# A mixer's channel projections as seven quadrant products over all 1024 steps, with the recurrences fed through DRAM

## The chip, the cores and the metric

The kernel runs on one core of one Trainium2 chip. The metric is the device time of one execution in microseconds; before the change three timed runs gave a median of 1631.3 us (1629.72 to 1633.17).

A core has five engines, each with an instruction queue of its own that it works through in order. TensorE (PE) multiplies matrices from SBUF into PSUM. VectorE (DVE) does arithmetic on tiles, ScalarE (ACT) activation functions and copies, GpSimd (POOL) small work. SyncE (SP) computes nothing here; it issues DMA transfers. The engines wait for one another on semaphores.

## What is computed

One layer of a hybrid decoder on a sequence of 1024 steps with 1024 channels, in float32:

```python
h = rms_norm(x, norm_mix)
proj = h @ w_in                                # 1024 x 8192
xa, ga, q, f, v, g, m_a, m_b = split(proj)     # 1024 channels each
xa = causal_depthwise_conv(xa, conv_w, conv_b)
y_a = rg_lru(xa) * gelu(ga)                    # recurrence h[t] = a[t] h[t-1] + u[t] per channel
o = rms_norm(hgrn2(silu(q), k(f), log_f(f), v), hg_norm)   # 8 heads, state 128 x 128
y_b = o * silu(g)
x = x + (sigmoid(m_a) * y_a + sigmoid(m_b) * y_b) @ w_out
x = x + square(relu(rms_norm(x, norm_mlp) @ w_up)) @ w_down
return rms_norm(x, norm_final)
```

Both recurrences run along the sequence. rg_lru has a 256-wide block matrix product for each of its two gates; hgrn2 works in blocks of steps with products of decay factors.

## The kernel before

**Precision.** Every float32 operand of a large product is split in two float32r tiles, a rounded part H (an ACT copy, L76) and the rest L (a DVE subtraction, L77). A product is then three matmuls, H·H, H·L and L·H (`mm3`, L115 to L117).

**Mixer.** The sequence is cut in two chunks c of T = 512 steps, the channels in four pairs p of two heads (256 channels). For each chunk `first_norm` normalises and transposes four row tiles into `hT`. Then for every pair come `project_v`, `project` of xa, `conv`, `project` of q and f, `rg_lru`, `hgrn` and `gates`, which projects g, mb, ga and ma and merges both branches into `ys`, kept in SBUF. `project` reads two weight tiles of 512 KB (`next_w`: one DMA on SP, one split) and makes 48 matmuls of 512 columns in two PSUM banks. `project_v` makes 96 matmuls of 256 columns. Results are read from PSUM directly by the recurrences, and the states `hcar`, `xcar` and `scar` carry over from the first chunk to the second. So each weight tile is loaded and split twice, once for a chunk. The output projection of the first chunk (`out_proj`, L599) runs between the chunks, that of the second beside `second_norm` after the mixer.

**MLP.** The up-projection already uses seven products in place of eight: a quadrant step of weights A (2 × 2 blocks) and activations B (2 × 2 blocks) is made of the seven products of `PLAN`, 12 matmuls each, with sums of the weights (`sums`, L759 to L762) and of the activations (`combos`, L666 to L669). The names t1, n2, T3 and T4 are such sums. This stage lies between about 1020 and 1310 us of the span, and its tiles are called uX, uY and uZ. The down-projection (dX, dY, dZ) follows to the end.

**Order.** The Tile framework writes the order of each engine's queue: ready instructions by priority, where the priority is the order of the program text, raised by `tc.high_priority`. A buffer that is used again makes the next writer wait for its last reader. All loads and stores of the mixer go through SP's queue, in order; the weight splits have a raised priority (400), rg_lru 300.

## Time and profile before

| | before |
|---|---|
| median of 3 runs | 1631.3 us |
| profiled execution | 1630.48 us |
| its span, first to last instruction | 1628.7 us |
| PE busy / instructions | 1584.9 us / 9240 |
| DVE busy / instructions | 1212.7 us / 1751 |
| ACT busy / instructions | 764.4 us / 1186 |
| POOL busy | 65.8 us |
| granted TensorE clock, mean | 0.996 |
| DMA | 246.51 MB, mean 151 GB/s |

A matmul's busy time runs from its start to the end of its pipeline, so neighbours overlap: what counts is the distance between two starts. The windows view gives each engine's busy time in a stretch of the span, with the number of instructions, the granted clock (1.00 is full speed) and the share of the DMA engines' time.

### The profile page before, as it was taken

What the parts mean: (1) busy time and instruction counts of PE and PEld (TensorE: products, weight loads), DVE (VectorE), ACT (ScalarE), POOL (GpSimd) and SP (SyncE); (2) the same over time, 40 slices, a digit from 0 to 9 for tenths busy, and PEclk for the clock granted to TensorE, in tenths of its full rate; (3) what the DMA queues carried; (4) which work ended last, traced back from release to release, by engine and by line L of the source; (5) the groups of instructions that cost most, each with busy time, mean ns of one, the idle gap of its engine ahead of it and who ended that gap; (6) DMA issues with size and microseconds to landing.
All of it is one profiled execution on the core that took longest, in us unless ns stands there. A gap on an engine that the chain in (4) does not pass through costs nothing.

```text
span 1628.7 us, 23177 instructions
## 1 busy us (share of the span) xinstructions
PE 1584.9 (97%) x9240; PEld 1303.1 (80%) x9240; DVE 1212.7 (74%) x1751; ACT 764.4 (47%) x1186; POOL 65.8 (4%) x99
## 2 busy tenths in 40 slices
PE   7999999999999999999999997999999999999998
PEld 6788788788788788787787876888878878888886
DVE  5975956848764865848759688977777888888876
ACT  4643545435442544436434566766776731222113
POOL 0010100100100000100100100000000000000000
PEclk9999999999999999999999998999999999999999
DMA  6212212122243222222122352666656575666652
GB/s 237 91 66 91 91 66 103 66 91 91 80 167 136 86 78 90 80 78 101 69 91 91 117 207 104 250 246 250 235 233 248 222 269 228 251 244 251 254 203 104
DMA packets 57996, 246.51 MB, mean 151 GB/s; under 512 B 6688, under 2 KB 6816, under 8 KB 47136
## 3 DMA queue, kind: packets, MB, share of 16 engines
q1 hardware_dynamic: 56304, 239.27, 39.3%
q10 hardware_dynamic: 1584, 5.77, 1.0%
q8 instruction: 72, 1.18, 0.3%
q14 instruction: 36, 0.29, 0.1%
HBM read 185.24 MB, written 59.77 MB: 150 GB/s over the span
## 4 chain that ended last, share of the span: by engine, by line
PE 80%; DVE 16%; DMA 2%; issue 1%; ACT 1%; POOL 0%; DVEq 0%; POOLq 0%; SPq 0%; ACTq 0%
PE dX L115 3%; PE uX L115 3%; PE uX L117 3%; PE uX L116 3%; PE dX L116 3%; PE dX L117 3%; DVE wL L77 2%; PE pj_ga L117 2%; PE pj_ga L116 2%; PE pj_ga L115 2%; PE pj_f L117 2%; PE pv L115 2%; PE pv L117 2%; PE pv L116 2%; PE pj_ma L117 2%; PE pj_ma L116 2%
## 5 line engine op out<-in xcount | busy, mean ns | idle before, releaser
L77 DVE TENSOR_TENSOR wL<-raw,wH 128x1024 fp32r<-128x1024 f32 x160 | 194.3, 1214 | 150.0 <-ACT wH L76 145.8
L76 ACT CAST wH<-raw 128x1024 fp32r<-128x1024 f32 x160 | 167.9, 1050 | 168.1 <-issue 66.4
L963 DVE TENSOR_TENSOR acc<-acc,dX 128x512 f32<-128x512 f32 x128 | 85.2, 684 | 31.2 <-PE dX L117 30.1
L76 ACT CAST wA<-q 128x512 fp32r<-128x512 f32 x32 | 19.8, 621 | 129.6 <-PE dX L117 103.7
L963 DVE TENSOR_TENSOR acc<-acc,dY 128x512 f32<-128x512 f32 x64 | 43.6, 686 | 17.3 <-PE dY L117 15.7
L345 DVE RECIPROCAL rr<-rr 128x512 f32<-128x512 f32 x16 | 53.5, 3347 | 0.0
L823 ACT ACTIVATE b<-b 128x512 f32<-128x512 f32 x48 | 30.2, 631 | 38.6 <-DVE b L822 38.5
L115 PE MATMUL pv<-wH,hT0H 128*128 128x256 f32 x128 | 37.4, 292 | 0.0
L116 PE MATMUL pv<-wL,hT0H 128*128 128x256 f32 x128 | 37.0, 289 | 0.0
L117 PE MATMUL pv<-wH,hT0L 128*128 128x256 f32 x128 | 37.0, 289 | 0.0
L115 PE MATMUL pv<-wH,hT1H 128*128 128x256 f32 x128 | 36.5, 285 | 0.0
L117 PE MATMUL pv<-wH,hT1L 128*128 128x256 f32 x128 | 36.2, 283 | 0.0
L116 PE MATMUL pv<-wL,hT1H 128*128 128x256 f32 x128 | 36.2, 283 | 0.0
L311 DVE SCALAR_TENSOR_TENSOR xc<-xp,pvt,xc 128x512 f32<-128x512 f32 x48 | 33.1, 746 | 0.0
L551 ACT ACTIVATE on<-po 128x128 f32<-128x128 f32 x64 | 17.0, 278 | 33.5 <-PE po L541 33.2
L570 ACT ACTIVATE smb<-pj_mb 128x512 f32<-128x512 f32 x16 | 9.6, 598 | 45.3 <-PE pj_mb L117 45.2
L824 ACT ACTIVATE b<-b 128x512 f32<-128x512 f32 x48 | 30.1, 630 | 1.1
L77 DVE TENSOR_TENSOR wA<-q,wA 128x512 fp32r<-128x512 f32 x32 | 22.0, 687 | 9.9 <-ACT wA L76 9.7
L444 POOL TENSOR_SCALAR seg<-seg 128x128 f32<-128x128 f32 (+1 forms) x16 | 14.5, 905 | 361.1 <-DVE seg L384 361.1
L565 ACT ACTIVATE g<-pj_g 128x512 f32<-128x512 f32 x16 | 9.6, 600 | 37.2 <-PE pj_g L117 37.2
L384 DVE TENSOR_TENSOR seg<-seg 128x128 f32<-128x128 f32 (+2 forms) x96 | 26.7, 307 | 0.2
L117 PE MATMUL pj_ga<-hT1H,wL 128*128 128x512 f32 x64 | 26.5, 414 | 0.0
(1854 smaller groups left out, 5261.5 us busy)
## 6 DMA issues: line engine op xcount, KB each, us to landing
raw<-wts_in SPq DMA_DIRECT2D x160, 512.0 KB, 3.4
q<-mlp_in SPq DMA_DIRECT2D x64, 512.0 KB, 3.9
x<-x_in SPq DMA_DIRECT2D x8, 512.0 KB, 6.1
acc<-x ACTq DMA_DIRECT2D x8, 512.0 KB, 6.1
y_out<-acc SPq DMA_DIRECT2D x16, 256.0 KB, 2.1
xs<-x_in SPq DMA_DIRECT2D x8, 256.0 KB, 3.5
x<-xs SPq DMA_DIRECT2D x8, 256.0 KB, 2.3
x2s<-x_in SPq DMA_DIRECT2D x4, 512.0 KB, 4.7
```

Of the source, the lines that this page charges most:

```text
L76: keep(A.copy(h, src))
L77: keep(V.tensor_tensor(out=lo, in0=src, in1=h.bitcast(F32), op=ALU.subtract))
L115: PE.matmul(o, ah, bh, start=first, stop=False, **how)
L116: PE.matmul(o, ah, bl, start=False, stop=False, **how)
L117: PE.matmul(o, al, bh, start=False, stop=last, **how)
L311: V.scalar_tensor_tensor(xc[:, s, :], xp[:, j : j + T], pvt[:, PV_CW + 8 * j + u : PV_CW + 8 * j + u + 1], xc[:, s, :], op0=ALU.mult, op1= ...
L345: V.reciprocal(rec, rec)
L384: mul = lambda o, a, b: V.tensor_tensor(out=o, in0=a, in1=b, op=ALU.mult)
L551: A.activation(on[:, 4 * s + n, :], po[:, n * P : (n + 1) * P], AF.Square, accum_out=ssq[:, 4 * s + n : 4 * s + n + 1])
L823: A.activation(b[:, at, :], b[:, at, :], AF.Relu, scale=-1.0 if at == 2 else 1.0)
L824: A.activation(b[:, at, :], b[:, at, :], AF.Square)
L963: V.tensor_tensor(out=dst, in0=dst, in1=banks[bk, pr], op=op)
```

## The change

The mixer no longer walks over chunks and pairs. All eight row tiles are normalised and transposed first; the two halves of the channels and of the steps make the quadrants B11, B21, B22 and B12, and `combos` makes t1, n2, T3 and T4 of them. The v projection is made for both chunks and both halves of its columns at once, in matmuls of 512 columns, and goes to DRAM.

The other seven projections become 28 quadrant products of the MLP's kind (`MIX`): a product takes 256 weight columns and all 1024 steps. XA(p) holds the two heads of xa of a pair, QF(u) holds q and f of one head, GM(u) g and mb, GA(u) ma and ga. The products of a head's gates come two heads later than its recurrence (`_mixer_quads`). Of the four weight sums two come out of DMA transfers: block A21 is loaded to SBUF by SP, and a DMA issued by POOL adds A22 or A11 to it (`added`); DVE makes the other two. The three banks of a product (X, Y, Z) all come from the four banks `pj`, which are read out at once: X after step 0 is copied to Z, and steps 1 and 2 are copied to SBUF.

What leaves PSUM goes to DRAM, head by head: raw xa, q and f (`raw_out`), the finished gates (`gate_a`, `gate_b`), the states of rg_lru (`h_d`) and the normalised outputs of hgrn (`o_d`). `gated_recurrence(p)` and `hgrn(u)` load their inputs from there and run over all 1024 steps, in single buffers that both share by tag (q1, qa, seg, f, kk, v, ks, scT). `merge(u)` loads the four results of a head, merges and splits them and stores `y_d`, which both output projections load again. The first one now stands after the mixer, ahead of the second.

In rg_lru the DVE reciprocal is replaced by an ACT exponential and two DVE steps, the first tap of the convolution moves from ACT to DVE, and in hgrn the scaling by the norm moves from DVE to ACT. Evictions and weight preparation have priority 1000. The pool `raw` has three buffers in place of four.

The diff, cut to its core:

```diff
+ROWS = {"XA": ("xa", "xa"), "QF": ("q", "f"), "GM": ("g", "mb"), "GA": ("ma", "ga")}
+def _mixer_quads():
+    todo = []
+    for p in range(NPAIR):
+        todo.append(("XA", p))
+        for u in (2 * p, 2 * p + 1):
+            todo.append(("QF", u))
+            if p > 0:
+                todo += [("GM", u - 2), ("GA", u - 2)]
+    return todo + [(kind, u) for u in (2 * NPAIR - 2, 2 * NPAIR - 1) for kind in ("GM", "GA")]
+MIX = _mixer_quads()
+UP = len(MIX)
+DOWN = UP + QUADS
...
+        def load(k):
+            if adding and k == 0:
+                raw[k] = pools[0].tile([P, 512], F32, tag="a11", name=f"q{i}{k}")
+                nc.sync.dma_start(raw[k], quads[i, k][:, 0:512])
+            else:
+                raw[k] = raws(f"q{i}{k}")
+                nc.sync.dma_start(raw[k], quads[i, k])
+        def added(k):
+            s[k] = raws(f"s{i}{k}")
+            nc.sync.dma_start(s[k][:, 0:512], halves(quads[i, 0])[1])
+            G.dma_start(s[k][:, 0:512], halves(quads[i, 1 - k])[1 - k], accum_op=ALU.add)
...
+        def sums():
+            a11, (a12, a22) = raw[0][:, 0:512], halves(raw[1])
+            if not adding:
+                s.update({k: raws(f"s{i}{k}") for k in range(2)})
+            (s1, s2), (s3, s4) = halves(s[0]), halves(s[1])
+            if not adding:
+                a21 = raw[0][:, 512:1024]
+                V.tensor_tensor(out=s1, in0=a21, in1=a22, op=ALU.add)
+                V.tensor_tensor(out=s3, in0=a21, in1=a11, op=ALU.add)
+            V.tensor_tensor(out=s2, in0=s1, in1=a11, op=ALU.add)
+            V.tensor_tensor(out=s4, in0=s2, in1=a12, op=ALU.add)
...
+    def transposed(r):
+        c, tt = divmod(r, 4)
+        b = st.tile([P, 2, T], F32, tag=f"b{c}", name=f"hraw{r}", bufs=4 if c == 0 else 1)
+        for h in range(2):
+            pt = bank("hg", f"xT_{r}_{h}")
+            for k in range(4):
+                PE.transpose(pt[:, k * P : (k + 1) * P], xns[r][:, (4 * h + k) * P : (4 * h + k + 1) * P], ident)
+            op_split(pt, f"B{h + 1}{c + 1}", tt)
+            keep(A.copy(b[:, h, :], pt))
+        if c == 0:
+            b0[tt] = b
+        else:
+            a = b0[tt]
+            combos(a[:, 0, :], a[:, 1, :], b[:, 1, :], b[:, 0, :])
+            for src, o in ((a[:, 0, :], "t1"), (b[:, 1, :], "n2"), (b[:, 0, :], "T3"), (a[:, 1, :], "T4")):
+                op_split(src, o, tt)
...
+                        mm3(pp[tt], hh[:, ku % 4, cut], hl[:, ku % 4, cut], wh[:, cols], wl[:, cols], ku == 0, ku == 7)
...
+        for tt in range(4):
+            vt = st.tile([P, 512], F32, tag="vt", name=f"vt{c}{hf}{tt}", bufs=2)
+            A.copy(vt, pp[tt])
+            nc.sync.dma_start(v_d[hf][:, :, 4 * c + tt, :], vt.rearrange("p (h d) -> p h d", h=4))
...
+    w_end[0] = 2 * V_TILES
+    project_v(0, 0, next_rows(4, 5))
+    project_v(0, 1, next_rows(6, 7))
+    project_v(1, 0, small_stuff)
+    project_v(1, 1, lambda: None)
+    for n in range(2):
+        work[n] = quad_steps(n, (w1m, wp), singles=1, adding=True)
+        for k in ("load0", "add0", "add1", "load1", "sums", "a", "b", "c") if n == 0 else ("load0", "add0", "add1"):
+            work[n][k]()
...
+    def gated_recurrence(p):
+        xp = [mt(t, f"xp{2 * p + s}", (P, 1792)) for s, t in enumerate(("q1", "qa"))]
         for s in range(2):
...
+            G.memset(xp[s][:, 0:3], 0.0)
+            nc.sync.dma_start(xp[s][:, 3 : S + 3], xa_d[2 * p + s])
+        wi = mt("v", f"wi{p}", (P, 2, T))
+        raw = wi.rearrange("p s t -> p (s t)")
+        nc.sync.dma_start(raw, wts[V_TILES + p])
+        wh, wl = (mt(t, f"rg{p}{t}", (P, 1024), F32R) for t in ("ks", "scT"))
+        split(raw, wh, wl)
...
-            V.reciprocal(rec, rec)
...
+                A.activation(e, w, AF.Exp, scale=sp4n[:, u : u + 1])
+                A.activation(w, w, AF.Tanh, scale=sp4[:, u : u + 1])
+            for s in range(2):
+                w, ig, e, t = parts[s]
+                V.tensor_scalar(w, w, 0.0, None, op0=ALU.max)
+                V.tensor_scalar(e, e, 1.0, None, op0=ALU.add)
+                V.scalar_tensor_tensor(t, w, 1.0, e, op0=ALU.add, op1=ALU.mult)
+                V.scalar_tensor_tensor(t, t, -4.0, e, op0=ALU.add, op1=ALU.mult)
+                V.tensor_scalar(e, t, -0.5, -1.0, op0=ALU.mult, op1=ALU.add)
...
+                V.scalar_tensor_tensor(w, w, -0.5, t, op0=ALU.mult, op1=ALU.mult)
+                V.tensor_tensor(out=ig, in0=ig, in1=w, op=ALU.mult)
+                h = w
+                V.tensor_tensor_scan(h, e, ig, hcar[:, u : u + 1], op0=ALU.mult, op1=ALU.add)
+                if c + 1 < NC:
+                    G.tensor_copy(hcar[:, u : u + 1], h[:, T - 1 : T])
+                nc.sync.dma_start(h_d[u][:, at : at + T], h)
...
+    def hgrn(u):
+        nm = f"{u}"
+        mul = lambda o, a, b: V.tensor_tensor(out=o, in0=a, in1=b, op=ALU.mult)
+        qr = mt("qa", f"qr{nm}", (P, 1792))[:, 0:S]
+        nc.sync.dma_start(qr, q_d[u])
+        f = mt("f", f"f{nm}", (P, S))
+        kk = mt("kk", f"kk{nm}", (P, S))
+        nc.sync.dma_start(f, f_d[u])
+        v = mt("v", f"v{nm}", (P, 8, P))
+        nc.sync.dma_start(v, v_d[u // 4][:, u % 4])
+        scT = mt("scT", f"scT{nm}", (P, 8, P))
+        G.memset(scT, 0.0)
+        seg = mt("seg", f"seg{nm}", (P, 1536))
+        dd = mt("dd", f"dd{nm}", (P, 8, 32))
+        A.activation(kk, f, AF.Sigmoid, scale=-1.0)
+        A.activation(f, f, AF.Sigmoid)
+        A.activation(seg[:, 0:S], qr, AF.Sigmoid)
+        V.tensor_scalar(f, f, omlb[:, u : u + 1], lb[:, u : u + 1], op0=ALU.mult, op1=ALU.add)
+        V.tensor_scalar(kk, kk, omlb[:, u : u + 1], None, op0=ALU.mult)
+        V.tensor_scalar(f, f, F_MIN, 1.0, op0=ALU.max, op1=ALU.min)
+        q1 = mt("q1", f"q1{nm}", (P, 1792))[:, 0:1536].rearrange("p (a b) -> p a b", b=3)
         r2 = lambda a: a.rearrange("p (a b) -> p a b", b=2)
...
+        mul(q1[:, :, 0:2], r2(seg[:, 0:S]), r2(qr))
...
-        mul(on, on, rs.unsqueeze(2).to_broadcast([P, 8, P]))
...
+                A.activation(on[:, n, :], po[:, n * P : (n + 1) * P], AF.Identity, scale=r[:, n : n + 1])
+            pt = bank("hg", f"poT{half}{u}")
+            for n in range(4):
+                PE.transpose(pt[:, n * P : (n + 1) * P], on[:, n, :], ident)
+            ot = m.tile([P, T], F32, tag="o", name=f"ot{half}{u}", bufs=1)
+            A.activation(ot, pt, AF.Identity, scale=pvt[:, PV_HG : PV_HG + 1])
+            nc.sync.dma_start(o_d[u][:, half * T : (half + 1) * T], ot)
...
+    def merge(u):
+        for c in range(NC):
+            at = slice(c * T, (c + 1) * T)
+            t = {}
+            for k, src in (("h", h_d), ("a", ma_d), ("o", o_d), ("b", mb_d)):
+                t[k] = ev.tile([P, T], F32R if k in "ab" else F32, tag="g", name=f"mg{k}{u}{c}", bufs=3)
+                nc.sync.dma_start(t[k].bitcast(F32) if k in "ab" else t[k], src[u][:, at])
+                if k in "ab":
+                    tf = t[k].bitcast(F32)
+                    V.tensor_tensor(out=tf, in0=tf, in1=t["h" if k == "a" else "o"], op=ALU.mult)
+            a, b = t["a"], t["b"]
+            af, bf = a.bitcast(F32), b.bitcast(F32)
+            V.tensor_tensor(out=af, in0=af, in1=bf, op=ALU.add)
+            A.copy(b, af)
+            V.tensor_tensor(out=a, in0=af, in1=bf, op=ALU.subtract)
+            nc.sync.dma_start(y_d[u, c][:, 0:T], bf)
+            nc.sync.dma_start(y_d[u, c][:, T : 2 * T], af)
...
+    def raw_out(n, step, o, dst):
+        t = ev_tile("t", f"r{step}_{n}", 4)
+        if step == 3:
+            A.copy(t, o)
+        elif step == 4:
+            V.scalar_tensor_tensor(t, o, -1.0, e_of.pop((n, 1)), op0=ALU.mult, op1=ALU.subtract)
+        elif step == 5:
+            V.tensor_tensor(out=t, in0=o, in1=e_of.pop((n, 2)), op=ALU.add)
         else:
...
+            A.activation(t, o, AF.Identity, scale=-1.0)
+        i, j = {3: (0, 0), 4: (1, 1), 5: (0, 1), 6: (1, 0)}[step]
+        nc.sync.dma_start(dst[i][:, j * T : (j + 1) * T], t)
...
+    def gate_b(n, u, step, o):
+        t = ev_tile("t", f"b{step}_{n}", 4)
+        if step == 3:
+            A.activation(t, o, AF.Sigmoid)
+            mul_to(t, t, o)
+            held[n, 0] = t
+        elif step == 4:
+            V.tensor_tensor(out=t, in0=o, in1=e_of.pop((n, 1)), op=ALU.add)
+            A.activation(t, t, AF.Sigmoid, scale=-1.0)
+            held[n, 1] = t
+        elif step == 5:
+            V.tensor_tensor(out=t, in0=o, in1=e_of.pop((n, 2)), op=ALU.add)
+            s = ev_tile("t", f"s{step}_{n}", 4)
+            A.activation(s, t, AF.Sigmoid)
+            mul_to(s, s, t)
+            mul_to(s, s, held.pop((n, 1)))
+            nc.sync.dma_start(mb_d[u][:, T : 2 * T], s)
+        else:
+            A.activation(t, o, AF.Sigmoid, scale=-1.0)
+            mul_to(t, t, held.pop((n, 0)))
+            nc.sync.dma_start(mb_d[u][:, 0:T], t)
+    def gate_a(n, u, step, o):
+        t = ev_tile("t", f"a{step}_{n}", 4)
+        root = 0.044715**0.5
+        if step == 3:
+            A.activation(t, o, AF.Sigmoid)
+            held[n, 0] = t
+        elif step == 4:
+            V.tensor_tensor(out=t, in0=o, in1=e_of.pop((n, 1)), op=ALU.add)
+            s = ev_tile("t", f"s{step}_{n}", 4)
+            A.activation(s, t, AF.Square, scale=root)
+            V.scalar_tensor_tensor(s, s, 1.0, t, op0=ALU.add, op1=ALU.mult)
+            A.activation(s, s, AF.Sigmoid, scale=-2.0 * GELU_C)
+            V.scalar_tensor_tensor(s, t, -1.0, s, op0=ALU.mult, op1=ALU.mult)
+            held[n, 1] = s
+        elif step == 5:
+            V.tensor_tensor(out=t, in0=o, in1=e_of.pop((n, 2)), op=ALU.add)
+            A.activation(t, t, AF.Sigmoid)
+            mul_to(t, t, held.pop((n, 1)))
+            nc.sync.dma_start(ma_d[u][:, T : 2 * T], t)
+        else:
+            A.activation(t, o, AF.Square, scale=root)
+            V.scalar_tensor_tensor(t, t, 1.0, o, op0=ALU.add, op1=ALU.mult)
+            A.activation(t, t, AF.Sigmoid, scale=-2.0 * GELU_C)
+            V.scalar_tensor_tensor(t, o, -1.0, t, op0=ALU.mult, op1=ALU.mult)
+            mul_to(t, t, held.pop((n, 0)))
+            nc.sync.dma_start(ma_d[u][:, 0:T], t)
+    def project(n, step):
+        kind, u = MIX[n]
+        bk, wo, ho = PLAN[step]
+        first = (n, bk) not in banks
+        if first:
+            banks[n, bk] = bank("pj", f"p{kind}{bk}{u}")
+        o = banks[n, bk]
+        wh, wl = ops_w[n][wo]
+        hh, hl = hop[ho]
+        for k in range(4):
+            cols = slice(k * P, (k + 1) * P)
+            mm3(o, wh[:, cols], wl[:, cols], hh[:, k, :], hl[:, k, :], first and k == 0, k == 3, not first)
+        with tc.high_priority(K_EV):
+            if step == 0:
+                banks[n, "Z"] = bank("pj", f"p{kind}Z{u}")
+                A.copy(banks[n, "Z"], o)
+            elif step < 3:
+                e_of[n, step] = ev_tile("e", f"e{step}_{n}", 2)
+                A.copy(e_of[n, step], o)
+            elif kind == "XA":
+                raw_out(n, step, o, (xa_d[2 * u], xa_d[2 * u + 1]))
+            elif kind == "QF":
+                raw_out(n, step, o, (q_d[u], f_d[u]))
+            else:
+                (gate_b if kind == "GM" else gate_a)(n, u, step, o)
...
+    for n, (kind, u) in enumerate(MIX):
+        if n + 2 < UP:
+            work[n + 2] = quad_steps(n + 2, (w1m, wp), singles=1, adding=True)
+        todo = {
+            0: [(n, "d")],
+            1: [(n + 1, "load1")],
+            3: [(n + 1, "sums"), (n + 1, "a"), (n + 1, "b"), (n + 2, "load0"), (n + 2, "add0")],
+            6: [(n + 1, "c"), (n + 2, "add1")],
+        }
+        for step in range(7):
+            project(n, step)
+            with tc.high_priority(K_PREP):
+                for i, k in todo.get(step, ()):
+                    if i < UP:
+                        work[i][k]()
+        if kind == "XA":
+            gated_recurrence(u)
+        elif kind == "QF":
+            hgrn(u)
+        elif kind == "GA":
+            merge(u)
...
+    def load_y(c):
+        ys = [ysp.tile([P, 2, T], F32R, tag="y", name=f"y{u}{c}", bufs=8) for u in range(8)]
+        for u in range(8):
+            nc.sync.dma_start(ys[u].rearrange("p a t -> p (a t)").bitcast(F32), y_d[u, c])
+        return ys
...
+    w_end[0] = len(seq)
+    ys = load_y(0)
+    for hf in range(2):
+        pp = out_proj(ys, hf, range(4), "0")
+        for tt in range(4):
+            cols = slice(hf * 512, (hf + 1) * 512)
+            xs = n2p.tile([P, D], F32, tag="xn", name=f"xs{tt}{hf}", bufs=2)[:, 0:512]
+            nc.sync.dma_start(xs, x[tt * P : (tt + 1) * P, cols])
+            V.tensor_tensor(out=xs, in0=pp[tt], in1=xs, op=ALU.add)
+            nc.sync.dma_start(x2d[tt][:, cols], xs)
+    ys = load_y(1)
...
```

702 lines of the change are left out of this document (294 added, 408 removed).

## The prediction

> **What bounds the kernel now.** I read the page's busy times and its chain of waits first:
>
> ```profile
> span 1628.7 us, 23177 instructions
> ...
> PE 1584.9 (97%) x9240; PEld 1303.1 (80%) x9240; DVE 1212.7 (74%) x1751; ACT 764.4 (47%) x1186; POOL 65.8 (4%) x99
> ...
> PE 80%; DVE 16%; DMA 2%; issue 1%; ACT 1%; POOL 0%; DVEq 0%; POOLq 0%; SPq 0%; ACTq 0%
> ```
>
> PE is busy nearly throughout and carries 80% of the chain; DVE is the only other engine on it. Then the windows view: the mixer, one of its eight rounds (a chunk and a pair), the hottest 20 us of a round, a stall after the mixer, and the up-projection:
>
> ```profile
> 11.00:930.00 919.00, 904.83 (x6302) 756.27 (x6302) 641.70 (x973) 424.86 (x698) 56.98 (x79) 1.00 0.27 95
> 69.20:176.70 107.50, 106.13 (x757) 88.93 (x756) 75.48 (x114) 49.89 (x83) 7.44 (x11) 1.00 0.25 84
> 80.00:100.00 20.00, 18.82 (x299) 14.79 (x300) 19.96 (x45) 6.98 (x11) 3.56 (x6) 1.00 0.18 64
> 980.00:1000.00 20.00, 13.94 (x57) 10.89 (x58) 18.39 (x29) 13.99 (x25) 2.27 (x3) 0.74 0.35 128
> 1030.30:1280.30 250.00, 250.00 (x1072) 200.51 (x1071) 200.64 (x247) 174.93 (x246) 0.00 (x0) 1.00 0.63 244
> ```
>
> Columns are length, then busy time and instructions of PE, weight loads, DVE, ACT, POOL, clock, DMA share, GB/s. The mixer is bound by PE (905 of 919 us), with DVE at 70%; only while a recurrence runs is DVE full (19.96 of 20), and PE still does 18.8, because projections that need no recurrence fill its queue. The last row matters most: the up-projection already works in seven products, with DVE and ACT at 80% and 70%, and PE has no gap. So PE's work is the first thing to count, and whether DVE leaves PE alone the second.
>
> **PE's work.** The timeline of PE gives the distance between two starts, here in the first and last rows of a run of 26 matmuls of 512 columns and of 29 matmuls of 256:
>
> ```profile
> 119.72 0.39 PE L116 MATMUL pj_ma<-hT0L,wH 128*128 128x512 f32 x1
> ...
> 125.39 0.39 PE L117 MATMUL pj_ma<-hT0H,wL 128*128 128x512 f32 x1
> ...
> 126.61 0.28 PE L116 MATMUL pv<-wL,hT0H 128*128 128x256 f32 x1
> ...
> 129.96 0.28 PE L117 MATMUL pv<-wH,hT0L 128*128 128x256 f32 x1
> ```
>
> 5.67/25 = 226.8 ns and 3.35/28 = 119.6 ns. The seven-product form is slower a matmul: 250/1072 = 233.2 ns in the up-projection's window. Counts by group:
>
> ```profile
> L117 PE MATMUL pj_ga<-hT1H,wL 128*128 128x512 f32 x64 | 26.5, 414 | 0.0
> L115 PE MATMUL pv<-wH,hT0H 128*128 128x256 f32 x128 | 37.4, 292 | 0.0
> ```
>
> Removed: 6 such groups of 64 for each of seven projections, 2688 x 0.2268 = 609.6 us. Added: 28 quadrants of 84 matmuls, 2352 x 0.2332 = 548.5 us. That is -61.1 us; at the old distance it would be -76.2. I take the up-projection's, since the form is the same. v: 768 x 0.1196 = 91.9 us become 384 x 0.2268 = 87.1, or 89.5 at 0.2332; I take -4. The gates' block products of rg_lru (192 matmuls), the blocks of hgrn, the transposes and both output projections keep their counts. **PE's work falls by 65 us, by 81 at most.**
>
> The Trainium skill ("TensorE: Matmul & The Clock Gate", "Wait — 56ns, not 53.3ns?") puts warm matmuls of 512 columns 215.7 ns apart; by it the 336 matmuls saved would be worth 72 us. The trace disagrees, with 226.8 and 233.2 ns at clock 1.00, so the rows decide.
>
> **DVE's work.** The rows that carry the prices:
>
> ```profile
> L77 DVE TENSOR_TENSOR wL<-raw,wH 128x1024 fp32r<-128x1024 f32 x160 | 194.3, 1214 | 150.0 <-ACT wH L76 145.8 <-PE pj_ga L117 2.6 <-PE xT_x L145 1.5
> L345 DVE RECIPROCAL rr<-rr 128x512 f32<-128x512 f32 x16 | 53.5, 3347 | 0.0
> L347 DVE TENSOR_TENSOR ri<-ri,xc 128x512 f32<-128x512 f32 x16 | 11.0, 686 | 0.0
> L384 DVE TENSOR_TENSOR on<-on,hrs 128x1024 f32<-128x1024 f32 x8 | 9.8, 1225 | 14.5 <-POOL hrs L557 14.5
> L376 DVE TENSOR_SCALAR f<-f,par 128x512 f32<-128x512 f32 x16 | 8.7, 541 | 0.0
> ```
>
> Weight splits of the mixer: 136 x 1.214 = 165 before; 28 x 3.5 + 16 (v) + 4 (rg) = 118 after, 143 us: -22. Weight sums on DVE: 56 x 0.686 = +38. Evictions of XA and QF: 24 x 0.686 = +16. Gates: a round had 10 operations of 512 columns, 4 of 1024 and a scalar one, about 12.5 us, 100 in all; after, 6 in `gate_b`, 8 in `gate_a` and 8 in `merge` for each head, 176 x 0.686 = 121: +21. Row tiles 4 to 7 get four sums and four splits more each: 32 x 0.686 = +22. Reciprocal: -53.5 + 32 x 0.686 = -31. First tap: 16 x 0.541 = +9, less 3 for the carried columns. Scaling of `on`: -10. Sum **+40 us**. The first output projection, 8 splits and 8 additions or 15 us, leaves the mixer with 192 x 0.2268 = 43.5 us of PE. So DVE has 641.7 + 40 - 15 = 667 us of work in a mixer whose PE work takes 919 - 65 - 43.5 = 810: 82%. That is the up-projection's load, where PE lost nothing.
>
> ACT, by these rows:
>
> ```profile
> L346 ACT ACT_TABLE_LOAD x16 | 20.5, 1283 | 0.3
> L819 ACT COPY e<-uX 128x512 f32<-128x512 f32 x32 | 18.4, 578 | 0.4 <-PE uX L117 0.4
> ```
>
> 84 copies of X, X and Y cost 49 us, the other evictions and repeated sigmoids some 30 more than the ones they replace, and rg_lru needs exp, tanh, sqrt and sigmoid; if each of its eight half-sequences reloads tables four times more, that is 41 us. 425 + 120 = 545 of 810, 67%: not the bound.
>
> **What does not lie beside other work.** (a) PE's first 53 us (9 to start, two halves of v at 22) must see eight row tiles ready; DVE needs 8 x 1.28 for the norms, 48 x 0.69 for their splits and sums and 10 weight splits of 1.21, 56 us in all, so that the last tile may come late: +3, between 0 and 10. (b) Quadrants in hot stretches: 18.8 of 20 us is what PE keeps when DVE is full. The round as a whole loses 1.4 of 107.5, which is in the 919 already; if every stretch were like the hot one, 6% of 549 us, 33. The up-projection's row gives 0. I take +9. (c) After GA7, `merge(7)` goes out and in again:
>
> ```profile
> xs<-x_in SPq DMA_DIRECT2D x8, 256.0 KB, 3.5
> x<-xs SPq DMA_DIRECT2D x8, 256.0 KB, 2.3
> ...
> raw<-wts_in SPq DMA_DIRECT2D x160, 512.0 KB, 3.4
> ```
>
> store 2.3, load 3.5, four operations 2.8, a copy 0.6, store 2.3, load of y 3.4: 15 us. The first output projection needs head 7 only after seven heads' matmuls, 7 x 12 x 0.227 = 19 us, so it hides if heads 0 to 6 are back in SBUF by then; their loads stand in SP's queue behind the merge's, which wait. +5, between 0 and 15. (d) The recurrences' chain, next paragraph: +10, between 0 and 80.
>
> **The chain of recurrences.** The buffers are single, so a pair's `gated_recurrence` and two `hgrn` follow each other. One round before, by DVE's timeline (first rounds), from convolution to gates, from gates to scan, and through hgrn:
>
> ```profile
> 43.85 0.74 DVE L311 SCALAR_TENSOR_TENSOR xc<-xp,pvt,xc 128x512 f32<-128x512 f32 x1
> ...
> 57.36 0.43 DVE L342 TENSOR_SCALAR rw<-rw 128x512 f32<-128x512 f32 x1 [2.26 <-ACT rw L338]
> ...
> 75.50 1.28 DVE L352 TENSOR_TENSOR_SCAN h<-rr,hcar,ri 128x512 f32<-128x512 f32 x1
> ...
> 79.39 0.86 DVE L384 TENSOR_TENSOR q<-q,f 128x512 f32<-128x512 f32 x1
> ...
> 110.64 0.16 DVE L555 TENSOR_SCALAR hssq<-hssq 128x8 f32<-128x8 f32 x1
> ```
>
> 13.5 + 19.4 + 31.4 = 64 us, of which about 12 are other work (ten splits by L77's 1.21) and 4 the saved part of two reciprocals: 48. A pair now needs two of these and three trips through DRAM (2.3 + 3.5): 114 us. PE needs 7 x 19.6 + 48 x 0.227 + 2 x 14 (107.5 less 336 and 96 matmuls and the rg block) = 176 us a pair. Preparation and evictions go ahead of the chain on DVE: seven quadrants of 5.7 and 23 us of gates and evictions, 63 of those 176 us. If they only fill its waits, a pair takes about 160; if all add, 114 + 63 = 177, and in the time in which no matmul of a recurrence slows the quadrants, up to 197. Starting at about 125, four pairs end between 765 and 913, PE's projections at about 790 to 805. So it is nearly even. I take 170, and 10 us of tail.
>
> **Sum**: -65 + 3 + 9 + 5 + 10 = -38; 1630.5 (the profiled execution: span 1628.7 and 1.8 around it) becomes **1592 us**. The median is 0.8 above that execution, which changes nothing here.
>
> **The rivals.** *Only PE counts*: everything hides as in the up-projection, and the sum is -65 to -81: 1550 to 1565, middle 1557. For it: 250 of 250 us at the same DVE load. Against it: there no chain of recurrences had to keep up. Chance 0.22.
>
> *The chain becomes the bound*: at 197 us a pair, 3.3 pairs are done when the projections run out near 780; the rest, 0.7 x 114 = 80 us, runs with PE nearly idle and ends at 860, some 55 late, and the output projection then starts cold, as the window at 980 does (0.74). 1630.5 - 65 + 17 + 55 + 5 = 1643. It costs more than the change saves once a pair takes over 190. For it: DVE at 82%, ACT's table loads, POOL's power function and queues in order lengthen each step. Against it: the hot row. Chance 0.20.
>
> *The weights come late*: A21 plus A22 is two transfers one after the other, about 7 us by the 256 KB row, in the 11 us between `add1` and `sums`; all loads share SP's queue with stores that wait for evictions, where before a load already waited long:
>
> ```profile
> SPq L84 <- DVE wL L77: 670.3, 132, 10.3
> ```
>
> No transfer issued by POOL is in the trace. From 0 (the slack holds) to 3 us a quadrant: 28 x 1.5 = 42 in the middle, 1634: no gain. Chance 0.13.
>
> The Trainium skill ("SBUF — State Buffer", "A bandwidth-pool intuition that's wrong (but worth ruling out)") says that a transfer issued by GpSimd waits for its descriptors while DVE holds the port that both share, 3.1 us in place of 0.62. By it each addition would come 2.5 us later, 1.5 of the 4 us of slack would be left, and this rival would be nearer 0.2; no run here shows such a transfer yet.
>
> **How the numbers follow.** The forecast has 0.45, its own range 1570 to 1620 from the bounds of (a) to (d). The range **1545 to 1650** takes in PE's floor at the old distance (1549) and the chain at 197. A difference under 0.2%, 3.3 us, can't be told from none. Faster: 0.45 + 0.22 + 0.05 from the lower parts of the rivals = 0.72; slower 0.22; same 0.06.
>
> **What would show it.** Quadrant matmuls 233 ns apart and 19.6 us a quadrant; v at 227 ns a matmul. PE above 95% from 11 us to the last GA; DVE near 82% there. `hgrn(7)` ends before GA7 if the forecast holds; a stretch of PE under 50% before the output projection, with DVE full, shows the chain. Waits of DVE or ACT on DMA for s or raw tiles show late weights. Wrong would be: DVE's sum off by over 60 us, since 100% is 143 us away, or PE's distance off by 10 ns, 24 us.

## The result, and the profile after

The changed kernel takes 1700.2 us (median of four runs, 1699.1 to 1703.4) against 1631.1 us before: a ratio of 1.043, 95% interval 1.041 to 1.044. It is slower by 69 us, where 38 us less was forecast. The forecast time, 1592 us, is 108 us off; 107 of these find their place below.

The page after, with the total busy times and the chain of waits:

```profile
span 1697.3 us, 22898 instructions
PE 1563.2 (92%) x8520; PEld 1242.5 (73%) x8520; DVE 1242.3 (73%) x1908; ACT 839.5 (49%) x1335; POOL 128.1 (8%) x169
PE 43%; DMA 11%; DVE 9%; ACT 4%; issue 3%; POOL 1%; SPq 0%; DVEq 0%; POOLq 0%; ACTq 0%
```

PE is busy for 22 us less than before (1584.9), where 65 were forecast; part of the difference is a lower granted clock, as the windows below show. Its share of the chain fell from 80% to 43%. DMA's rose from 2% to 11% and ACT's from 1% to 4%, while DVE's fell from 16% to 9%; the shares of the line add up to 71%, and the rest is not named in it. The windows view by stages, after: the v projection, the 28 quadrants with the recurrences, the stretch from the last gate to the up-projection, the up-projection. The last row is the same for one quadrant without a recurrence beside it.

```profile
9.00:119.90 110.90, 101.70 (x448) 79.85 (x449) 69.88 (x121) 60.75 (x99) 7.00 (x10) 1.00 0.48 152
119.90:919.40 799.50, 726.10 (x4936) 572.46 (x4935) 580.92 (x989) 427.15 (x738) 114.36 (x141) 0.97 0.52 156
919.40:1052.70 133.30, 105.99 (x443) 84.77 (x441) 73.52 (x96) 50.73 (x75) 4.87 (x7) 0.89 0.71 248
1052.70:1375.60 322.90, 316.10 (x1342) 251.59 (x1341) 257.77 (x322) 220.57 (x312) 0.55 (x1) 0.99 0.58 220
833.20:852.80 19.60, 19.60 (x85) 15.79 (x84) 9.81 (x14) 8.07 (x12) 1.81 (x2) 1.00 0.62 183
```

and before, from the last gate to the up-projection:

```profile
926.80:988.50 61.70, 53.24 (x255) 43.38 (x254) 54.49 (x75) 41.33 (x65) 5.93 (x7) 0.94 0.60 217
```

In the 800 us of the quadrants PE is idle for 73 us. What it waits for there, as total, times and longest:

```profile
PE poT L702 <- ACT on L699: 13.2, 11, 2.4
PE sc L536 <- DVE q L506: 13.1, 4, 6.1
PE pr L126 <- ACT xcH L87: 11.3, 5, 4.9
PE sc L536 <- DVE qb L506: 6.9, 4, 3.8
PE sc L621 <- DVE qb L506: 6.7, 4, 2.2
PE pGAX L126 <- DVE a L781: 5.6, 4, 2.6
```

Five of these six are matmuls of a recurrence (hgrn's blocks and outputs, rg_lru's gates) whose operand DVE or ACT had not finished. The sixth is a quadrant that waits for its bank to be read out. None of PE's waits in this window is a quadrant that waits for its weights. And what DVE waits for in the same window:

```profile
DVE s L252 <- DMA s<-quads_in: 50.4, 21, 5.2
DVE s L253 <- DMA q<-quads_in: 24.6, 19, 4.5
```

These are the two weight sums, 75 us. The first (L252) waits for an addition by transfer; the wait of the second (L253) is put down to the plain load of q. The timeline of DVE shows one of them in its place (start, duration, line, operation, and in brackets the idle time before it):

```profile
549.41 1.22 DVE L88 TENSOR_TENSOR ws315L<-s,ws315H 128x1024 fp32r<-128x1024 f32 x1
553.80 0.69 DVE L252 TENSOR_TENSOR s<-s,q 128x512 f32<-128x512 f32 x1 [3.17 <-DMA s<-quads_in]
554.41 0.42 DVE L484 TENSOR_SCALAR xp<-xp 128x512 f32<-128x512 f32 x1
554.74 0.69 DVE L496 TENSOR_TENSOR wi<-wi 128x512 f32<-128x512 f32 x1
...
557.68 1.28 DVE L498 TENSOR_TENSOR_SCAN wi<-xc,hcar,wi 128x512 f32<-128x512 f32 x1
...
565.83 1.22 DVE L88 TENSOR_TENSOR ws116L<-s,ws116H 128x1024 fp32r<-128x1024 f32 x1
```

The sum for quadrant 16 (553.80) is needed by the split at 565.83, 12 us later. DVE stands still for 3.17 us in front of it until the transfer of s lands, with rg_lru's next steps and its scan (L484, L496, L498) queued behind. Over the 28 quadrants the first sum stands 18.6 us ahead of DVE's half of its split in the median (6.6 to 33.7). ACT's half, which reads the sum first, begins 16.0 us after it.

### The profile page after: what moved, and what is told of

Same layout as the page of the kernel before. It is cut to its first block, busy times and chain, and to the rows that moved or that the text cites. A ratio compares the mean times of both kernels' runs of the same rounds, so it can differ in the third digit from the quotient of the medians.

```text
span 1697.3 us, 22898 instructions
## 1 busy us (share of the span) xinstructions
PE 1563.2 (92%) x8520; PEld 1242.5 (73%) x8520; DVE 1242.3 (73%) x1908; ACT 839.5 (49%) x1335; POOL 128.1 (8%) x169
## 4 chain that ended last, share of the span: by engine, by line
PE 43%; DMA 11%; DVE 9%; ACT 4%; issue 3%; POOL 1%; SPq 0%; DVEq 0%; POOLq 0%; ACTq 0%
PE dX L126 3%; PE dX L128 3%; PE dX L127 3%; PE uX L126 3%; PE uX L127 3%; PE uX L128 3%; DMA q<-quads_in 3%; DMA s<-quads_in 2%; PE dY L128 2%; PE dY L126 2%; PE dY L127 2%; PE uY L128 2%; PE uY L126 2%; PE uY L127 2%; DMA raw<-wts_in 1%
## 5 line engine op out<-in xcount | busy, mean ns | idle before, releaser
L241 POOL DMA_DIRECT2D s<-quads_in x56 | 51.5, 920 | 441.0 <-DMA s<-quads_in 124.9
L252 DVE TENSOR_TENSOR s<-s,q 128x512 f32<-128x512 f32 x60 | 41.4, 689 | 56.4 <-DMA s<-quads_in 51.7
L87 ACT CAST wH<-raw 128x1024 fp32r<-128x1024 f32 x40 | 42.0, 1051 | 66.1 <-PE po L127 30.1
L88 DVE TENSOR_TENSOR wL<-raw,wH 128x1024 fp32r<-128x1024 f32 x40 | 48.9, 1223 | 34.8 <-ACT wH L87 34.4
L126 PE MATMUL po<-wH,y 128*128 128x512 f32 x128 | 53.2, 421 | 18.7 <-DMA y<-yd 8.6
L253 DVE TENSOR_TENSOR s<-s,q 128x512 f32<-128x512 f32 x60 | 41.3, 688 | 29.7 <-DMA q<-quads_in 29.5
L88 DVE TENSOR_TENSOR wA<-q,wA 128x512 fp32r<-128x512 f32 x60 | 41.2, 686 | 20.5 <-ACT wA L87 20.5
L1124 DVE TENSOR_TENSOR acc<-acc,dY 128x512 f32<-128x512 f32 x64 | 43.5, 686 | 16.3 <-PE dY L128 15.3
L127 PE MATMUL po<-wL,y 128*128 128x512 f32 x128 | 53.3, 416 | 0.3 <-DVE wL L88 0.3
L128 PE MATMUL po<-wH,y 128*128 128x512 f32 x128 | 52.2, 408 | 0.0
L126 PEld LDWEIGHTS po<-wH,y 128*128 128x128 f32 x128 | 25.5, 200 | 26.0 <-DMA y<-yd 9.0
L127 PEld LDWEIGHTS po<-wL,y 128*128 128x128 f32 x128 | 26.0, 203 | 6.5 <-DVE wL L88 1.3
L702 PE MATMUL poT<-ident,on 128*128 128x128 f32 x64 | 18.4, 313 | 13.2 <-ACT on L699 13.2
L128 PEld LDWEIGHTS po<-wH,y 128*128 128x128 f32 x128 | 25.9, 202 | 5.5
L506 DVE TENSOR_TENSOR kk<-kk,seg 128x768 f32<-128x768 f32 (+1 forms) x32 | 26.9, 840 | 3.2 <-PE sc L639 3.2
```

The source lines that it names most:

```text
L87: keep(A.copy(h, src))
L88: keep(V.tensor_tensor(out=lo, in0=src, in1=h.bitcast(F32), op=ALU.subtract))
L126: PE.matmul(o, ah, bh, start=first, stop=False, **how)
L127: PE.matmul(o, ah, bl, start=False, stop=False, **how)
L128: PE.matmul(o, al, bh, start=False, stop=last, **how)
L241: G.dma_start(s[k][:, 0:512], halves(quads[i, 1 - k])[1 - k], accum_op=ALU.add)
```

## The experiments

All times are beside the kernel before on the same chip, 1630 to 1631 us. Each comes from a single execution unless a median is given. Eleven executions of one kernel below lie between 1622.2 and 1630.8 us, so two single times that are less than 10 us apart are not told apart. "Ahead" always means the median distance from the start of the first sum to DVE's half of its split. "Quadrants" is the time from the first matmul of the first quadrant to the last of the last; 799.5 us in the changed kernel.

**Without the recurrences.** In the main loop the two calls are taken out, and `merge` reads other tensors of the same shape:

```diff
-        if kind == "XA":
-            gated_recurrence(u)
-        elif kind == "QF":
-            hgrn(u)
-        elif kind == "GA":
+        if kind == "GA":
```

> Leaves out both recurrences (gated_recurrence and hgrn are not called; the merge reads raw xa and q in place of their results). What stays is the v projection, the 28 quadrants with all their weight preparation, the gates, the merge and everything behind. Theory A (TensorE's queue is in order, and matmuls of the recurrences whose inputs are late hold the quadrants behind them: 61 of the 73 us of PE waits between 120 and 918 us stand at such matmuls) expects the quadrants at 19.6 us each, 28 x 19.6 + 12 = 561 us from the first to the last in place of 798, and so about 1460 us in all. Theory B (the weight sums come late by themselves, 76 us of DVE waits at L252 and L253) expects the quadrants to stay at 21.5 us or more and the waits on s and q of DVE to stay near 70 us: 600 us or more for the 28, 1500 us or more in all.

Measured: 1491.2 us, quadrants 592 us. The window of the quadrants, then DVE's waits in it:

```profile
120.00:712.00 592.00, 564.96 (x2353) 447.41 (x2352) 270.11 (x351) 212.74 (x312) 46.67 (x53) 0.98 0.60 163
```

```profile
DVE s L253 <- DMA q<-quads_in: 83.7, 27, 6.2
DVE s L252 <- DMA s<-quads_in: 78.8, 26, 4.9
```

Neither expectation holds alone. DVE waits 162 us for transfers at the sums with little else to do, and the quadrants lose 43 us against 28 x 19.6 = 549; the 27 us in which PE is idle are all waits for DVE to read a bank. The rest of the 250 us that the changed kernel has above 549 is the recurrences' own matmuls, and 46 us that only both together cost: 799.5 - 592 = 207.5, of which 161 are PE's additional busy time (726.1 less 565.0).

**The sums on DVE.** The accumulating transfers go; DVE adds instead:

```diff
-            G.dma_start(s[k][:, 0:512], halves(quads[i, 1 - k])[1 - k], accum_op=ALU.add)
-            if not adding:
-                a21 = raw[0][:, 512:1024]
-                V.tensor_tensor(out=s1, in0=a21, in1=a22, op=ALU.add)
-                V.tensor_tensor(out=s3, in0=a21, in1=a11, op=ALU.add)
+            a21 = (s1, s3) if adding else (raw[0][:, 512:1024],) * 2
+            V.tensor_tensor(out=s1, in0=a21[0], in1=a22, op=ALU.add)
+            V.tensor_tensor(out=s3, in0=a21[1], in1=a11, op=ALU.add)
```

> The accumulating transfers that POOL issues are gone: SyncE loads A21 into both sum tiles as before, and DVE adds A22 and A11 (56 more operations of 0.69 us, 38 us of DVE). Theory B (the late accumulation holds DVE in order at the sums, and with it the recurrences' work behind) expects DVE's waits on transfers of s and q to fall from 76 us to under 35, PE's idle time between the first XA and the last GA from 73 us to 15 to 45, and a time of 1640 to 1675 us. Theory A without B (the recurrences' own chain of DVE, ACT and POOL steps is what comes late) expects no gain: 38 us more of DVE in the chain's way, 1700 to 1725 us.

Measured: 1639.8 us, 60 us less than the changed kernel, with 56 operations more for DVE, 38 us by the price of one. The window of the quadrants, then DVE's waits for s and q in it:

```profile
120.00:859.50 739.50, 706.87 (x4936) 559.04 (x4936) 612.10 (x1043) 428.01 (x738) 76.09 (x86) 1.00 0.45 149
```

```profile
DVE s L248 <- DMA q<-quads_in: 7.3, 7, 2.5
DVE s L249 <- DMA s<-quads_in: 6.3, 7, 2.6
```

DVE's waits fall from 75 to 14 us, PE's idle time from 73 to 33 us, and the same 4936 matmuls take 19 us less of busy time at a granted clock of 1.00 in place of 0.97: with 41 us of gaps went 19 us of slow clock. But this edit does two things. The second transfer goes, and the additions now wait for the tile q, so that the sums stand later in DVE's queue: the first is 3.0 us ahead of its split (the second 12.8, where it was 17.8). It does not tell whether the transfer or the place of the sum was at fault.

**The recurrences later.** Each call stands one quadrant later:

```diff
+    due, LATE = [], 6
...
         for step in range(7):
             project(n, step)
+            if step == LATE:
+                while due:
+                    due.pop(0)()
...
         if kind == "XA":
-            gated_recurrence(u)
+            due.append(lambda u=u: gated_recurrence(u))
         elif kind == "QF":
-            hgrn(u)
+            due.append(lambda u=u: hgrn(u))
```

> Each recurrence is written one quadrant later in the program, behind the seven steps of the next quadrant, so that its loads and matmuls stand later in every queue than the planner had them; nothing else changes. Theory A expects fewer waits of PE at recurrence matmuls (61 us to about 30), as their inputs have 20 us more: about 1670 us, if the last recurrence then still ends before the last quadrant. If the order is not the point but each step's inputs come late against its predecessor in the same chain (the lag moves along with the chain), nothing changes: 1690 to 1710 us.

Measured: 1702.3 us, quadrants 798 us. The recurrences did move (the last transposes of an hgrn output start at 848.7 us in place of 827.2), the time did not: PE is still idle for 75 us, and DVE still waits 78 us at the sums. That PE's queue holds matmuls whose operands are late is how the loss shows; this run gives no sign that it comes from there.

**The norms ahead.**

```diff
     rows(0)
     fill_w(1)
     load_x(2)
+    rows(1)
     transposed(0)
-    rows(1)
     fill_w(2)
     load_x(3)
+    rows(2)
     transposed(1)
-    rows(2)
+    rows(3)
     transposed(2)
-    rows(3)
     fill_w(3)
     transposed(3)
...
             for r in rs:
                 load_x(r)
                 rows(r)
+            for r in rs:
                 transposed(r)
```

> Of the eight row tiles, the norm of the next one is written ahead of the transposes of the one before it (in the program order that ACT and DVE are held to), so that square, norm, transposes and splits of two tiles overlap. Theory C (the 20 us that the v stage came late, 120 against some 100 us, lie in this serial chain, 7.7 us a tile with ACT and DVE half idle) expects the first quadrant 10 to 14 us earlier, near 107 us, and 1686 to 1692 us in all. The rival, that the splits of the weights or the matmuls themselves set the pace, expects less than 3 us: 1697 to 1703 us.

Measured: 1695.0 us, between the two ranges; the first quadrant starts at 116.4 in place of 119.9. The chain costs 4 us, not 10 to 14. Most of the 20 us that this expectation wanted to explain were no loss: 384 matmuls of 228 ns, 64 transposes and a start like the one before fill the stage, as the prediction had it.

**No addition at all.** The accumulating transfer is left out, and nothing takes its place.

```diff
-            G.dma_start(s[k][:, 0:512], halves(quads[i, 1 - k])[1 - k], accum_op=ALU.add)
```

> Leaves out the 56 accumulating transfers and puts nothing in their place: both sum tiles hold A21 alone, so the weights s1 to s4 are other numbers than the kernel needs, with the same operations on them. Against the run in which DVE makes these two sums (1639.8 us), it tells what DVE's 38 us cost there. If DVE's load lies beside PE's work (612 of 739 us, 83%), it is within 5 us of that run, 1633 to 1642. If DVE in its order is what now holds the recurrences, it is faster by a good part of the 38 us: 1605 to 1625.

Measured: 1648.7 us, outside both ranges: 51 us less than the changed kernel, and 9 us more than with the 56 additional operations of DVE. Taking that work off DVE brought nothing, so DVE's load is not what counts here. The sum again stands early, 21.9 us ahead of its split, but the sums wait only for plain loads, 26 us in all. In the changed kernel, a sum waits for two transfers in a row, by the first two of these medians from issue to landing:

```profile
s<-quads_in SPq DMA_DIRECT2D x56, 256.0 KB, 2.8
s<-quads_in POOLq DMA_DIRECT2D x56, 256.0 KB, 4.4
q<-quads_in SPq DMA_DIRECT2D x28, 256.0 KB, 4.5
```

The third line is a plain load of the same size, no faster than the accumulating one. So the runs show what the second transfer in the row costs, and not that an accumulating transfer is slow by itself.

**Two steps more.** Sums, splits, loads and additions are written two steps later:

```diff
-        for k in ("load0", "add0", "add1", "load1", "sums", "a", "b", "c") if n == 0 else ("load0", "add0", "add1"):
+        for k in ("load0", "add0", "add1", "load1", "sums", "a", "b", "c") if n == 0 else ("load0", "add0"):
...
         todo = {
-            0: [(n, "d")],
+            0: ([(n, "c")] if n else []) + [(n, "d"), (n + 1, "add1")],
             1: [(n + 1, "load1")],
-            3: [(n + 1, "sums"), (n + 1, "a"), (n + 1, "b"), (n + 2, "load0"), (n + 2, "add0")],
-            6: [(n + 1, "c"), (n + 2, "add1")],
+            5: [(n + 1, "sums"), (n + 1, "a"), (n + 1, "b"), (n + 2, "load0"), (n + 2, "add0")],
         }
```

> The accumulating transfers stay on POOL, but the sums of the next quadrant and the first two splits are written at step 5 in place of 3, the loads and additions that follow them two steps later too, and the splits of s3 and s4 at the first step of their own quadrant: from the issue of the second addition to the sums there are five steps, 14 us, in place of four, 11. If the gain of the sums on DVE came from time (two transfers one after the other plus POOL's issue do not fit in 11 us), DVE's waits on s and q fall from 76 us by a third or more, and the time to 1650 to 1680 us. If it came from the ring of three raw buffers (each tile is loaded when the one before it is split, so that everything moves along), nothing changes: 1690 to 1710 us.

Measured: 1713.2 us, 3 us above the second range, and DVE's waits for s and q are 88 us, not fewer than 75. The place in the text gives the sum no time: it still stands 18.4 us ahead of its split. This spoke for the ring of raw buffers (three tiles that are used in turn, each loaded when an earlier one has been split), so the ring was changed by itself.

**Four raw tiles.** The recurrences are left out, for room, and the ring is one tile longer:

```diff
-        return wp.tile([P, 1024], F32, tag="raw", name=name, bufs=3)
+        return wp.tile([P, 1024], F32, tag="raw", name=name, bufs=4)
```

> Both recurrences left out as in no_rec (their buffers are what makes room), and the ring of raw weight tiles four deep in place of three, 4 KB a partition more; accumulating transfers on POOL as in the changed kernel. Theory R (a raw tile is loaded at the moment in which the split of the tile three places before it frees its buffer: load, accumulation, sum and split stand in one closed ring, so no load is ever ahead) expects DVE's waits on s and q in the 28 quadrants to fall from 168 us to under 90, and the quadrants from 592 us to 555 to 570: 1455 to 1470 us in all. Rival T (two transfers one after the other take longer than the place in the program gives them, whatever the buffers) expects 585 to 592 us for the quadrants and 1485 to 1492 us in all.

Measured: 1487.6 us, quadrants 580 us. DVE's waits:

```profile
DVE s L252 <- DMA s<-quads_in: 131.5, 26, 7.3
DVE s L253 <- DMA q<-quads_in: 44.4, 22, 4.4
```

176 us, not fewer than the 162 with three tiles. The quadrants take 12 us less but begin 8 us later (at 128.2), and the whole gains 3.6 us, which is too little to be told from nothing. So the theory falls: the loads come earlier, and the sums move up with them (20.6 us ahead of the split in place of 10.9). That fits a planner which puts a sum where it takes its transfer to be done. The next run fixes the place.

**The sums tied to step 3.** The transfers stay; the sums take a factor of 1.0 that is made of step 3's product:

```diff
...
-            V.tensor_tensor(out=s2, in0=s1, in1=a11, op=ALU.add)
-            V.tensor_tensor(out=s4, in0=s2, in1=a12, op=ALU.add)
+            if adding and i > 0:
+                one = gates.pop()
+                V.scalar_tensor_tensor(s2, s1, one, a11, op0=ALU.mult, op1=ALU.add)
+                V.scalar_tensor_tensor(s4, s2, one, a12, op0=ALU.mult, op1=ALU.add)
...
+                if step == 3 and n + 1 < UP:
+                    gates.append(const.tile([P, 1], F32, tag="gate", name=f"one{n}", bufs=2))
+                    V.tensor_scalar(gates[0], banks[n, "Z"][:, 0:1], 0.0, 1.0, op0=ALU.mult, op1=ALU.add)
```

> The changed kernel with its accumulating transfers, and one thing more: the two sums that DVE makes for the next quadrant multiply by a 1.0 that is made of the finished product of step 3, so that they can't stand in DVE's queue ahead of that step, where the text has them (28 small DVE operations more, no other edit). Theory P (the planner takes the two transfers to be done sooner than they are and puts the sums, at priority 1000, right behind them, some 20 us before the split needs them, so that DVE waits in order with the recurrences behind it) expects DVE's waits on s and q to fall from 76 us to under 30 and a time of 1640 to 1665 us. If the transfers really come too late for the splits, the waits stay and the weights come later still: 1700 to 1730 us.

Measured: 1653.4 us, as its theory P expected. The window of the quadrants, then DVE's longest waits between 120 and 870 us:

```profile
121.00:875.60 754.60, 703.76 (x4938) 557.37 (x4938) 586.12 (x1015) 431.34 (x741) 109.80 (x141) 0.99 0.56 164
```

```profile
DVE xc L490 <- ACT xc L485: 20.8, 8, 4.3
DVE mga L722 <- DMA mga<-mad: 17.2, 7, 6.5
DVE mgb L722 <- DMA mgb<-mbd: 13.1, 6, 4.2
```

No wait for s or q is among DVE's waits of 2 us or more in that window. The accumulating transfers are all there, so they are in time for the weights; only DVE had been made to wait for them. POOL still issues every one of them, so its queue is not where most of the loss was. That the planner takes the transfers for shorter than they are is argued from this; what the plan assumed is in no trace. The sum now stands 2.2 us ahead of its split. Four runs make a table of two by two:

| | sum early (18.6 and 21.9 us ahead) | sum late (2.2 and 3.0 us ahead) |
|---|---|---|
| accumulating transfer | 1700.2 us, DVE waits 75 us | 1653.4 us |
| plain transfers alone | 1648.7 us, DVE waits 26 us | 1639.8 us, DVE waits 14 us |

Either remedy alone brings 47 to 52 us, and both together 60, though the run at the lower right also has 56 additions more on DVE. Most of the loss needs both the early place and the second transfer.

**The sums without their priority.**

```diff
-            with tc.high_priority(K_PREP):
-                for i, k in todo.get(step, ()):
-                    if i < UP:
+            for i, k in todo.get(step, ()):
+                if i < UP:
+                    with tc.high_priority(K_PREP if k != "sums" else 0):
                         work[i][k]()
```

> The changed kernel, with the sums alone taken out of priority 1000: they are written at the same place with the priority of the program text. If it is the raised priority that puts the sums ahead of the recurrences' work in DVE's queue, DVE's waits on s and q fall under 40 us and the time to 1640 to 1670 us, as with the sums tied to step 3 (1653.4 us). If it is the planner's idea of when the two transfers are done (DVE is free at that moment in its plan, whatever the priority), nothing changes: 1690 to 1710 us.

Measured: 1683.9 us, between the two ranges: the waits for s and q are still 69 us and the sum stands 13.4 us ahead. The raised priority accounts for 16 of the 47 us that tying the sums brought.

**A faster way to the end.** With the sums on DVE and the norms ahead, the first output projection is reordered:

```diff
+    first_proj(0, range(7))
+    first_proj(1, range(4))
     for hf in range(2):
-        pp = out_proj(ys, hf, range(4), "0")
+        first_proj(hf, range(4, 8) if hf else (7,))
+        pp = pps[hf]
```

`first_proj` holds the matmuls of `out_proj`, with the banks of the second half in `sc` and `hg`.

> The two sums on DVE (1639.8 us) and the norms ahead of the transposes (5 us less when done alone), and the first output projection in another order: heads 0 to 6 of its first half, heads 0 to 3 of its second half in the four other banks, then head 7 and the rest, so that 30 us of matmuls in place of 19 stand before the last head is needed. If the stretch from the last gate to the up-projection is long (131 us against 105 before) because head 7's way through DRAM takes some 30 us, the wait of 8.4 us for y and the cold clock behind it go, and the time is 1615 to 1626 us. If the stretch is set by the second norm's chain behind it (stores of x2, loads, norms), the gain is given back there: 1630 to 1637 us.

> The same kernel as dve_v_tail, timed in five rounds: 1623 to 1627 us, a ratio to before of 0.995 to 0.998, if its one look was typical; if it was a lucky one, 1628 to 1633 us and no difference from before that can be told.

Measured: 1624.7 us in a single execution, and 1627.1 us as the median of eleven, a ratio to before of 0.9976, interval 0.9966 to 0.9987. This version is 73 us faster than the changed kernel and level with the one before: 0.24% less, which the interval tells from nothing, but only just. Its median lies between the two outcomes of the first expectation and just above the upper edge of the lower one of the second. The stretch from the last gate to the up-projection fell from 131 us, with the sums on DVE alone, to 125. The wait for y is gone, and another stands in its place:

```profile
PE po L126 <- ACT wH L87: 14.2, 1, 14.2
```

SyncE's timeline shows that weight load (L95) behind loads of y for the second projection and behind the stores (L939) and loads (L937) of the first one's results:

```profile
903.04 0.86 SPq L868 DMA_DIRECT2D y<-yd  x2
907.09 1.03 SPq L939 DMA_DIRECT2D x<-xs  x2
912.01 0.86 SPq L95 DMA_DIRECT2D raw<-wts_in  x2
```

The stores wait for DVE's additions, here as total, times and longest between 880 and 925 us; the loads of y wait for PE for only 0.2 us in that time:

```profile
SPq L939 <- DVE xs L938: 13.5, 7, 4.8
```

**Those weights on another queue.**

```diff
-        nc.sync.dma_start(raw, wts[i])
+        (nc.sync if i < V_TILES else nc.scalar).dma_start(raw, wts[i])
```

> As dve_v_tail (1624.7 us), but the weights of both output projections are loaded by ACT's queue in place of SyncE's, where the last ones stood for 14 us behind loads of y that wait for TensorE. If that queue is the cause of the 14.2 us wait of TensorE for the weights and of the cold clock behind it: 1608 to 1616 us. If the transfers themselves are the limit there (298 to 353 GB/s between 890 and 920 us), the wait goes to y or x and the time stays at 1620 to 1626 us.

Measured: 1631.2 us, the median of ten, ratio to before 1.001 (0.9995 to 1.0025), above both ranges. The wait of 14.2 us is gone and its place is taken again:

```profile
PE xT_h L902 <- DVE xn_h L150: 8.6, 3, 5.0
PE po L127 <- DVE wL L88: 5.5, 2, 5.1
```

The stretch is 122 us long, 3 less, and the total got no better. What sets this stretch was moved twice and not settled. The DMA engines are busy for 0.85 to 0.95 of the time between 890 and 920 us in the version before this one, so the transfers themselves stay a rival that no run tests.

## Why the prediction was wrong, step by step

**PE's work** was right. A quadrant alone takes the 19.60 us that were worked out (84 matmuls, 233 ns each), and with the sums on DVE, at clock 1.00, PE is busy in the quadrants for 706.9 us where the sum has 704. Two rows of the v projection, with sixteen distances between them:

```profile
91.00 0.39 PE L127 MATMUL pv<-wL,hB22H 128*128 128x512 f32 x1
94.66 0.39 PE L128 MATMUL pv<-wH,hB22L 128*128 128x512 f32 x1
```

3.66/16 = 229 ns, between the two distances used. The rule of the Trainium skill ("TensorE: Matmul & The Clock Gate", "Wait — 56ns, not 53.3ns?"), 215.7 ns, does not hold here either.

**DVE's work** was right: 69.9 + 580.9 = 651 us up to the last gate against 667 worked out. ACT's 488 us were put too high, at 545. Neither engine is the bound; the share of DVE in the quadrants is 73%, and at 83% (the sums on DVE) the kernel is 60 us faster.

**(a) The v stage** was right: 11 + 106 (what the sum leaves beside four times 176 us) + 3 = 120; the first quadrant starts at 119.9, and writing the norms ahead took 3.5 us of that away.

**(b) and (d), and the rival of late weights: here it failed.** The sum gave the quadrants 704 + 9 + 10 = 723 us; they took 799.5. Of these 76 us, 45 to 60 go when the wait of the sums is taken away in one way or the other. With the sums on DVE the quadrants take 739.5 us, 16 above the forecast and inside the bounds of (d); where these 16 come from is open.

The step that failed is that the sum puts the wait for the additions at nothing. The prediction had the mechanism as a rival: two transfers in a row, about 7 us. That length was right: from SyncE's load of s to POOL's issue are 3.5 us in the median, and from there to the first sum 4.3. But it counted them against 11 us "between `add1` and `sums`", which is a distance in the text, and the planner does not keep it. 22 of the 28 first sums start 4.0 to 4.5 us after the issue of their addition, that is, right behind the transfer, and two steps more in the text gained nothing. So DVE waits for the transfers, wherever the text puts the two.

It also had another payer in mind. The rival prices what a quadrant loses for lack of weights, and names waits of DVE on transfers for s as the sign. The sign came, but the weights were in time; the price was paid by the recurrences queued behind DVE. Its size, 45 to 60 us or 1.6 to 2.1 us a quadrant, lies inside the rival's 0 to 3, a little above its middle of 1.5. The rival was nearly right in size, then, and had 0.13 of the chances; the forecast left it out. The two signs of being wrong that the prediction named, DVE's sum and PE's distance, did not show: the error lay in neither.

The Trainium skill ("SBUF — State Buffer", "A bandwidth-pool intuition that's wrong (but worth ruling out)") gives 3.1 us in place of 0.62 for a transfer that GpSimd issues beside a DVE copy; the estimate from it was 2.5 us more for each addition. No run here shows such a delay: the additions land 1.6 us later than the plain loads of s, but the medians of the plain transfers of that size go from 2.0 to 4.5 us in this kernel.

**The chain as the bound**, the rival of 1643 us, did not happen in its form. It expected the recurrences to end last, with PE nearly idle beside them. After the change, the first convolution and the last transposes of an hgrn output stand at 145 and 827 us:

```profile
L441 DVE TENSOR_SCALAR xc<-xp,pvt x16: 536/543/549, 145.3 to 697.5; 128x512 f32<-128x512 f32 x16
L702 PE MATMUL poT<-ident,on x64: 270/328/476, 272.3 to 827.2; 128*128 128x128 f32 x64
```

So the last recurrence ends 92 us before the last gate, and 682/4 = 170 us a pair is what (d) assumed. What failed is that PE's quadrants did not fill all the time beside the recurrences.

**(c) The end of the mixer** was too cheap. About 107 us were forecast (61.7 + 43.5 + 5, less the 3 us by which the mixer's window to 930 reaches into the stretch from 926.8) and 133.3 measured, 26 more. The way of head 7, by the timelines of PE, SyncE and DVE, after:

```profile
919.44 0.39 PE L128 MATMUL pGAX<-hT4H,wA1227L 128*128 128x512 f32 x1
923.39 0.32 SPq L799 DMA_DIRECT2D mad<-a  x1
927.66 0.38 SPq L714 DMA_DIRECT2D mga<-mad  x1
931.96 0.69 DVE L717 TENSOR_TENSOR mga<-mga,mgh 128x512 f32<-128x512 f32 x1 [2.81 <-DMA mga<-mad]
932.68 0.32 SPq L714 DMA_DIRECT2D mgb<-mbd  x1
935.42 0.69 DVE L717 TENSOR_TENSOR mgb<-mgb,mgo 128x512 f32<-128x512 f32 x1 [1.63 <-DMA mgb<-mbd]
938.24 0.32 SPq L724 DMA_DIRECT2D yd<-mga  x1
941.23 0.42 SPq L869 DMA_DIRECT2D y<-yd  x1
947.70 0.80 PE L126 MATMUL po<-wH,y 128*128 128x512 f32 x1 [8.62 <-DMA y<-yd]
```

28.3 us pass from the last gate's matmul to the first that uses head 7, where 15 were worked out and 19 were the cover. The term that was mis-sized is this trip of 15 us. It left out the operations between the last matmul and the gate's store (4.0 us), and the load of mgb, which stands behind the first product because `merge` has three buffers for its four loads (2.7). And it took four transfers as short as before: 4.3 us in place of 2.3 from the gate's store to its load, 4.3 in place of 3.5 for that load, 3.0 in place of 2.3 from the store of y to its load, and 6.5 in place of 3.4 for the load of y. Together these are the 13 us. The 8.6 us wait is a third of the 26; after it the two projections and the second norms follow each other, with PE idle for 27 us in the whole stretch and a clock of 0.89. The two runs that took one wait away each found the next; this part stays open.

**The up-projection**, which the change does not touch, took 322.9 us against 317.3 before (988.5 to 1305.8), 5.6 more. It was not forecast; no run was made for it, and it is 318.7 in the profile of the version with the faster way to the end.

Sum: 76 + 26 + 6 = 108 us, less 1 us by which the down-projection was shorter: 107 us, by which the profiled execution (1699.1 us) lies above the forecast. The median is 1 us above that execution.

## What to carry to other kernels

Where a planner writes the order, a distance between two lines of the text is no slack: look in the timeline at how far ahead of its user an instruction stands, and at what it waits for. An instruction that is placed as early as its transfer allows stops everything behind it on its engine; a dependency on the step at which it is wanted costs 27 small operations and was worth 47 us here. And a price of a late operand is not what its own user loses, but what is queued behind the wait.
